# Two output-norm weights moved from every block's gate into the rows of the output projection

## The chip, the cores and the metric

The kernel runs on one core of one Trainium2 chip, in one launch. The metric is the device time of that launch in microseconds (us). The engines of the core are named as the profile names them: PE (matrix products and transposes; PEld is its weight load), DVE (vector engine), ACT (activation engine), POOL (general engine) and SP, whose queue issues this kernel's DMAs.

## The reference, cut to what matters

One hybrid decoder layer over 4096 rows of width 1024. Eight attention heads of width 64 attend in three dilated windows; four heads of width 128 run a gated linear recurrence. Both halves are normalised head by head, multiplied by a norm weight of width 512, gated with silu, joined, and multiplied by `w_out`.

```python
proj = _rmsnorm(x, mix_norm_w) @ w_in
aq, ak, av, ag, hq, hf, hi, hg = split(proj)          # 512 columns each
attn = _longnet_mixture(aq, ak, av)                   # windows (128,1), (512,4), (2048,16)
rec = _hgrn2_chunked(silu(hq), 1 - f, hi, log(f))     # f from hf
y_attn = _head_rmsnorm(attn, attn_out_norm_w, 8) * silu(ag)
y_hgrn = _head_rmsnorm(rec, hgrn_out_norm_w, 4) * silu(hg)
mixed = concatenate([y_attn, y_hgrn], axis=-1)
x = x + mixed @ w_out
return _rmsnorm(x, final_norm_w)
```

A weight that multiplies column c of `mixed` can as well multiply row c of `w_out`.

## The kernel before, in words

`NB` is 32 blocks of 128 rows. Every full-precision product is made of three products of split operands: a high part rounded by ACT (names `hi`, `whi`, `xs`, `ph`) and the rest, `lo`, by DVE or POOL.

Stage 1 (from the start to about 746 us) projects x onto the columns of attention, in two passes P=0 and P=1 over 16 pairs of blocks. `plain_w` and `summed_w` load and combine the weights of a pass, `load_unit` the rows of a pair, and `plain_products` and `unit_rows` form a 2x2 block product from seven `half` products (L725 to L727) with sums on DVE in between (L752 to L763; u2, u4, C0 and C1 are their results). `attn_rows` then, for each block, rotates q and k, splits v, transposes q and k, and makes the gate: `e` is silu of the gate columns, multiplied at L286 by `gv`, a copy of the attention norm weight on all partitions (tile gvA, loaded by a DMA at L787 once for each pass), and written to `sg_d`.

Stage 2 (746 to about 2286 us) projects onto the columns of the recurrence. `for g in range(4, 8)` goes over its four heads and, inside, 16 pairs of blocks; `project_T` and `project_N` make the products (L201), `hgrn_gates`, `hgrn_values` and `hgrn_pair` the recurrence. `hgrn_values` ends with the gate's silu and, at L340 on POOL, a product with `hvec[0]` (tile gv0H, loaded at L295 for each head). Between these steps `take(left + rate)` draws pieces from the generator `attention()`: for each of eight heads the passes d=16, d=4 and d=1, each made of scores (L425, L426), exponentials (L436, L438), transposes (`flip`, L448 to L452), products with v (`weigh`, L460) and, after the pass d=1, `finish`, which reads back the gates from `sg_d`.

Behind that, in the order of the program: the loads of a half of `w_out` (`split_wo` on eight pieces of 128x512, L860 and L861); the rest of attention (`take(10 ** 9)`); 12 early products of the output projection (L878 to L892, `AHEAD`), which need the recurrence's half of `mixed` alone; then stage 3 (about 2398 us to the end): `load_y` reads `mixed` back and transposes it, `summed_wo` loads `w_out` whole (eight pieces `r[j]` of 128x1024 in tile xr, four buffers) and combines it into T1 to T4 and B22 through `split_wo`, and `begin`, `finish_pair` and `final_norm` make the output. T2, T1, T3 and T4 lie in the buffers of QS, KH, KL and OA, which attention's last head reads and writes.

The order in which the instructions stand on each engine is not that of the program. A scheduler plays the program through a modelled timeline and emits each engine's instructions in the order that comes out, bounded by the number of buffers of each tile (`bufs=`). An edit in one place can so move instructions in others.

Of the kernel before, what the change touches and what calls it, by code (L numbers as in the profile page):

```python
# [17 lines left out]
F32 = mybir.dt.float32  # L18
F32R = mybir.dt.float32r
I32 = mybir.dt.int32  # L20
U8 = mybir.dt.uint8
AF = mybir.ActivationFunctionType
ALU = mybir.AluOpType
# [7 lines left out]
KT = 8  # L31
# [4 lines left out]
C1 = 6.28125  # L36
# [13 lines left out]
def layer(ctx: ExitStack, tc: tile.TileContext, x, xT, xP, pos, w_in, w_out, nw, anw, hnw, lbraw, fnw,  # L50
          ident_in, mask_in, trih_in, invf_in, out):
    nc = tc.nc
    V, A, G, T = nc.vector, nc.scalar, nc.gpsimd, nc.tensor
# [16 lines left out]
    mask = const.tile([128, 3, 256], F32, name="mask")  # L70
    caus = const.tile([128, 128], U8, name="caus")
    nwt = const.tile([128, KT], F32, name="nwt")
    nnwt = const.tile([128, KT], F32, name="nnwt")
    mid = ExitStack()
    wp = mid.enter_context(tc.tile_pool(name="wp", bufs=8))
# [7 lines left out]
    rstdn = const.tile([128, NB], F32, name="rstdn")  # L83

    dma(nwt, nw)
    V.tensor_scalar(nnwt, nwt, -1.0, None, op0=ALU.mult)

    def rotary_tables():
# [162 lines left out]
        A.activation(e, e, AF.Ln)  # L251
        A.activation(e, e, AF.Exp, scale=-1.0)

    def attn_rows(P, b, C, gv):

        bs = slice(b * 128, (b + 1) * 128)
        t2 = p1p.tile([128, 2, 4, 16], F32, name="rot")
        c = C[:, :, 0:256].rearrange("p g (q e) -> p g q e", q=4)
        for n in range(2):
            sn = rsin[:, b : b + 1, 8 * n : 8 * n + 8].unsqueeze(1).to_broadcast([128, 2, 4, 8])  # L260
            V.tensor_mul(t2[:, :, :, 8 * n : 8 * n + 8], c[:, :, :, 8 - 8 * n : 16 - 8 * n], sn)
        c16 = c[:, :, :, 0:16]
        V.tensor_mul(c16, c16, rcos[:, b : b + 1, :].unsqueeze(1).to_broadcast([128, 2, 4, 16]))
        V.tensor_add(c16, c16, t2)
        hl = p1p.tile([128, 2, 2, 128], F32R, name="hl")
        rv = C[:, :, 256:384].rearrange("p g (q e) -> p g q e", q=2)
        V.tensor_copy(hl[:, :, :, 0:64], rv)
        G.tensor_tensor(hl[:, :, :, 64:128], rv, hl[:, :, :, 0:64].bitcast(F32), op=ALU.subtract)
        for g in range(2):
            dma(v_d[2 * P + g][bs], hl[:, g].bitcast(F32))  # L270
        pt_ = ps_x.tile([128, 512], F32, name="tr")
        for g in range(2):
            for q in range(2):
                T.transpose(pt_[:, g * 256 + q * 128 : g * 256 + (q + 1) * 128], C[:, g, q * 128 : (q + 1) * 128], ident)
        st = p1p.tile([128, 2, 4, 128], F32R, name="stk")
        p4 = pt_.rearrange("p (g n c) -> p g n c", g=2, n=2)
        A.activation(st[:, :, 0:2], p4, AF.Copy)
        V.tensor_sub(st[:, :, 2:4], p4, st[:, :, 0:2].bitcast(F32))
        for g in range(2):
            dma(qk_d[2 * P + g][:, :, bs], st[:, g].bitcast(F32))  # L280

        e = p1p.tile([128, 2, 128], F32, name="sg")
        A.activation(e, C[:, :, 384:512], AF.Exp, scale=-1.0)
        sigm(e)
        V.tensor_mul(e, e, C[:, :, 384:512])
        V.tensor_mul(e, e, gv)  # L286
        dma(sg_d[bs, P * 256 : (P + 1) * 256], e.rearrange("p g c -> p (g c)"))


# [1 line left out]

    def load_vec(pool, p):
        c = slice(p * 128, (p + 1) * 128)
        v0 = pool.tile([128, 128], F32, name="gv0H", bufs=1)
        dma(v0, hnw[:, c].partition_broadcast(128))  # L295
        v1 = pool.tile([128, 2], F32, name="gv1", bufs=2)
        dma(v1[:, 0:1], omlb_d[:, c].rearrange("o c -> c o"))
        V.tensor_scalar(v1[:, 1:2], v1[:, 0:1], -1.0, None, op0=ALU.mult)
        return v0, v1

    def hgrn_gates(t, ps):

        omlb, nomlb = hvec[1][:, 0:1], hvec[1][:, 1:2]
        rb = hp.tile([128, 256], F32, name="hrb", bufs=1)
        dma(rb, rstd_d[:, t * 256 : (t + 1) * 256].partition_broadcast(128))
        z = hp.tile([128, 2, 256], F32, name="hz", bufs=1)
        e = hp.tile([128, 2, 256], F32, name="he", bufs=1)
        V.tensor_tensor(z, ps.rearrange("p (a c) -> p a c", a=2), rb.unsqueeze(1).to_broadcast([128, 2, 256]), op=ALU.mult)  # L308
        A.activation(e, z, AF.Exp, scale=-1.0)
        sigm(e)  # L310
        G.tensor_tensor(z[:, 1], z[:, 1], e[:, 1], op=ALU.mult)
        cum = hp.tile([128, 256], F32, name="hcum", bufs=1)
        A.activation(cum, e[:, 0], AF.Ln, scale=nomlb, bias=1.0)
        V.tensor_tensor_scan(cum, keep, cum, 0.0, op0=ALU.mult, op1=ALU.add)
        c2 = cum.rearrange("p (n c) -> p n c", n=2)
        V.scalar_tensor_tensor(c2, c2[:, :, 127:128].to_broadcast([128, 2, 128]), -0.5, c2, op0=ALU.mult, op1=ALU.add)
        ea = hp.tile([128, 256], F32, name="hea", bufs=2)
        A.activation(ea, cum, AF.Exp)
        A.activation(cum, cum, AF.Exp, scale=-1.0)
        qd = hp.tile([128, 256], F32, name="hqd", bufs=2)  # L320
        G.tensor_tensor(qd, z[:, 1], ea, op=ALU.mult)
        kd = hp.tile([128, 256], F32, name="hkd", bufs=2)
        V.scalar_tensor_tensor(kd, e[:, 0], omlb, cum, op0=ALU.mult, op1=ALU.mult)
        return qd, kd, ea

    def hgrn_values(t, ps):

        n0 = 2 * t % 4
        if n0 == 0:
            hst["gv"] = hp.tile([128, 4, 256], F32, name="hgv", bufs=2)  # L330
            hst["ss"] = hp.tile([128, 4], F32, name="hss", bufs=2)
        gv = hst["gv"][:, n0 : n0 + 2]
        for n in range(2):
            b = 2 * t + n
            A.activation(gv[:, n], ps[:, 256 * n : 256 * (n + 1)], AF.Copy, scale=rstdn[:, b : b + 1])
        e = hp.tile([128, 2, 128], F32, name="heg", bufs=1)
        A.activation(e, gv[:, :, 0:128], AF.Exp, scale=-1.0)
        sigm(e)
        G.tensor_tensor(gv[:, :, 0:128], gv[:, :, 0:128], e, op=ALU.mult)
        G.tensor_tensor(gv[:, :, 0:128], gv[:, :, 0:128], hvec[0].unsqueeze(1).to_broadcast([128, 2, 128]), op=ALU.mult)  # L340

    def hgrn_pair(hh, t, qd, kd, ea):

# [396 lines left out]
        A.activation(C0[:, 0], pa, AF.Copy, scale=rstd[:, 2 * t : 2 * t + 1])  # L740
        return u2, pe

    def unit_rows(P, t, X, W, gv, C0, begun):
        u2, pe = begun
        b0, b1 = 2 * t, 2 * t + 1
        C1 = p1p.tile([128, 2, 512], F32, name="C", bufs=3)
        if pe is None:
            pe = ps_m.tile([128, 512], F32, name="m")
            half(pe, X["S4"], W["B22"])
        pb = ps_m.tile([128, 512], F32, name="m")  # L750
        half(pb, X["S2"], W["T2"])
        V.tensor_tensor(u2, pb, u2, op=ALU.add)  # L752
        pc = ps_m.tile([128, 512], F32, name="m")
        half(pc, X["S1"], W["T1"])
        u4 = p1p.tile([128, 512], F32, name="u4", bufs=1)
        V.tensor_tensor(u4, pc, u2, op=ALU.add)
        V.tensor_tensor(C0[:, 1], pe, u4, op=ALU.add)
        A.activation(C0[:, 1], C0[:, 1], AF.Copy, scale=rstd[:, b0 : b0 + 1])
        pd = ps_m.tile([128, 512], F32, name="m")
        half(pd, X["S3"], W["T3"])  # L760
        V.tensor_tensor(C1[:, 1], pd, u4, op=ALU.add)
        half(pd, X["A22"], W["T4"], start=False)
        V.tensor_tensor(C1[:, 0], pd, u2, op=ALU.add)  # L763
        A.activation(C1, C1, AF.Copy, scale=rstd[:, b1 : b1 + 1])
        attn_rows(P, b0, C0, gv)
        attn_rows(P, b1, C1, gv)

    def row_tile():
        return p1p.tile([128, 2, 512], F32, name="C", bufs=3)
# [12 lines left out]
    for P in range(2):  # L782
        if P:
            W = {"B11": plain_w(1, 0), "B21": plain_w(1, 1)}
            summed_w(1, W)
        gv = p1p.tile([128, 2, 128], F32, name="gvA", bufs=1)
        dma(gv, anw[:, P * 256 : (P + 1) * 256].rearrange("o (g c) -> o g c", g=2).partition_broadcast(128))  # L787
        early = None
        for t in range(NB // 2):
            if not P and t != 1:  # L790
# [8 lines left out]
            if (P, t) == (0, 0):  # L799
                row_stats(1)  # L800
                C0n = row_tile()
                early = C0n, plain_products(1, Xn, W, C0n, third=False)
            unit_rows(P, t, X, W, gv, C0, begun)
            X = Xn
            if (P, t) == (0, 3):
                lower_bounds()
# [33 lines left out]
    X = load_pair(0, 4)  # L840
# [15 lines left out]

    def split_wo(raw, hi, lo):
        A.activation(hi, raw, AF.Copy)  # L860
        V.tensor_sub(lo, raw, hi.bitcast(F32))  # L861
        return hi, lo

    WO = {}
    for j in range(2):
        WO[f"B{j + 1}1"] = []
        for k in range(4 * j, 4 * j + 4):
            raw = xp.tile([128, 512], F32, name="raw", bufs=3)
            dma(raw, w_out[k * 128 : (k + 1) * 128, 0:512])
            WO[f"B{j + 1}1"].append(split_wo(raw, wp.tile([128, 512], F32R, name="whi", bufs=8),  # L870
                                             wp.tile([128, 512], F32R, name="wlo", bufs=8)))
    three.close()
    fp = two.enter_context(tc.tile_pool(name="fp", bufs=1))
    fnwt = fp.tile([128, D], F32, name="fnwt", bufs=1)
# [118 lines left out]
    def summed_wo():  # L993
        bt = {n: big.tile([128, S], F32R, name="w" + n, tag=tag) for n, tag in (("T2", "QS"), ("T1", "KH"), ("T3", "KL"), ("T4", "OA"))}
        WO.update({n: [None] * 4 for n in ("T1", "T2", "T3", "T4", "B22")})
        for k in range(4):
            r = [fp.tile([128, D], F32, name="xr", bufs=4) for _ in range(2)]
            for j in range(2):
                dma(r[j], w_out[(4 * j + k) * 128 : (4 * j + k + 1) * 128, :])
            b11, b12, b21, b22 = r[0][:, c0], r[0][:, c1], r[1][:, c0], r[1][:, c1]  # L1000

            def unit(name, src):
# [78 lines left out]
```

## Time and profile before

| what | value |
|---|---|
| three runs | 2721.2, 2730.94, 2735.6 us; median 2730.94 |
| the profiled execution: its time, its span | 2725.64 us, 2723.9 us |
| mean granted PE clock | 0.968 of full speed |
| busy PE, DVE, ACT, POOL | 2559.8, 2042.7, 1743.4, 1066.0 us |
| DMA, share of 16 engines | 60.1% |

The span runs from the first to the last instruction that the profile shows; 1.7 us of the execution lie around it. The busy times are sums over the whole span, with stages of different limits in it. Times in the rows below are in us from the start of the span; a row of windows has the window, its length, then for PE, PEld, DVE, ACT and POOL the busy time with the number of instructions, the granted PE clock, the share of DMA engines busy, and GB/s.

### The profile page before, as it was taken

The numbers are of one execution on the slowest core, as the hardware profiler recorded it, in microseconds if no ns is written. First come the engines' busy times: TensorE is split into PE (matmuls) and PEld (weight loads), VectorE is DVE, ScalarE is ACT, GpSimd is POOL, SyncE is SP. The second block draws the span as 40 slices with busy tenths as digits, with TensorE's granted clock in tenths as the row PEclk, the third lists the DMA queues.
The fourth block names the chain that finished last, engine by engine and source line by source line (L and its number), as shares of the span: only waits on it lengthen the run. The fifth ranks groups of instructions, "written<-read, shape, count | busy, mean of one in ns | idle before, by whom it ended". The sixth has DMA issues, their size and how long they took to land. (4 is left out here: it accounts for less than half of the span.)

```text
span 2723.9 us, 52124 instructions
## 1 busy us (share of the span) xinstructions
PE 2559.8 (94%) x17186; PEld 2310.5 (85%) x17186; DVE 2042.7 (75%) x5322; ACT 1743.4 (64%) x4811; POOL 1066.0 (39%) x1012
## 2 busy tenths in 40 slices
PE   5899989999979999999999899999899999889998
PEld 4678867888879989899999799999899998668886
DVE  8787788777637788777787787677787877867875
ACT  8755565555548768768667677577678677534443
POOL 5455646665434364142242141231231331144443
PEclk8999999999979999999999899999999998999999
DMA  6864463444686775774774764764855753645553
GB/s 230 257 180 143 150 205 114 150 147 143 184 271 185 222 244 175 201 188 135 199 202 143 214 178 136 208 173 148 239 168 151 227 160 103 202 151 181 182 159 109
DMA packets 459106, 487.44 MB, mean 179 GB/s; under 512 B 120105, under 2 KB 335189, under 8 KB 458837
## 3 DMA queue, kind: packets, MB, share of 16 engines
q1 hardware_dynamic: 458836, 484.12, 60.1%
q8 instruction: 137, 2.24, 0.3%
q14 instruction: 133, 1.08, 0.1%
HBM read 354.45 MB, written 129.52 MB: 178 GB/s over the span
## 5 line engine op out<-in xcount | busy, mean ns | idle before, releaser
L201 PE MATMUL proj<-xs,whi 128*128 128x256 f32 x2048 | 432.1, 296 | 20.9 <-ACT whi L163 12.3
L201 PE MATMUL proj<-whi,xs 128*128 128x256 f32 x2048 | 431.9, 293 | 3.7 <-DVE hz L308 3.7
L201 PEld LDWEIGHTS proj<-xs,whi 128*128 128x128 f32 x2048 | 333.9, 194 | 27.2 <-ACT whi L163 13.7
L201 PEld LDWEIGHTS proj<-whi,xs 128*128 128x128 f32 x2048 | 335.3, 193 | 5.3 <-DVE hz L308 3.9
L436 DVE CUSTOM_DVE_ANT_0 pt<-att,mask 128x256 f32<-128x256 f32 (+1 forms) x768 | 269.2, 387 | 76.4 <-PE att L426 74.6
L201 PE MATMUL proj<-xs,wlo 128*128 128x256 f32 x1024 | 302.0, 295 | 0.3 <-DVE wlo L164 0.3
L201 PE MATMUL proj<-wlo,xs 128*128 128x256 f32 x1024 | 299.9, 293 | 0.0
L452 DVE TENSOR_TENSOR pl<-att,ph 128x512 fp32r<-128x512 f32 (+1 forms) x384 | 237.4, 624 | 55.4 <-ACT ph L451 53.0
L438 ACT ACTIVATE pt<-pt,ml 128x256 f32<-128x256 f32 (+1 forms) x512 | 238.1, 467 | 55.3 <-DVE ml L436 54.2
L451 ACT ACTIVATE ph<-att 128x512 fp32r<-128x512 f32 (+1 forms) x384 | 203.4, 542 | 50.5 <-PE po L460 24.3
L448 PE MATMUL att<-ident,pt 128*128 128x128 f32 x1368 | 227.7, 279 | 4.2 <-ACT pt L438 3.0
L460 PE MATMUL po<-ph,vh 128*128 128x128 f32 (+1 forms) x856 | 211.9, 277 | 8.4 <-ACT ph L451 2.6
L460 PE MATMUL po<-pl,vh 128*128 128x128 f32 (+1 forms) x856 | 206.4, 287 | 1.3 <-DVE pl L452 1.2
L201 PEld LDWEIGHTS proj<-xs,wlo 128*128 128x128 f32 x1024 | 199.0, 194 | 2.1 <-issue 1.2
L201 PEld LDWEIGHTS proj<-wlo,xs 128*128 128x128 f32 x1024 | 198.0, 193 | 1.2 <-issue 1.0
L460 PEld LDWEIGHTS po<-ph,vh 128*128 128x128 f32 x856 | 166.5, 194 | 13.0 <-issue 5.4
L466 ACT ACTIVATE pot<-po 64x512 f32<-64x512 f32 (+1 forms) x256 | 124.2, 485 | 73.7 <-DVE o L570 34.2
L725 PE MATMUL m<-tw,ss 128*128 128x512 f32 x384 | 155.0, 404 | 16.9 <-ACT tw L172 6.6
L448 PEld LDWEIGHTS att<-ident,pt 128*128 128x128 f32 x1368 | 161.7, 143 | 9.6 <-ACT pt L438 5.0
L460 PEld LDWEIGHTS po<-pl,vh 128*128 128x128 f32 x856 | 167.0, 195 | 2.8 <-DVE pl L452 2.3
L726 PE MATMUL m<-tw,ss 128*128 128x512 f32 x384 | 154.9, 404 | 4.7 <-DVE tw L173 4.7
L727 PE MATMUL m<-tw,ss 128*128 128x512 f32 x384 | 155.9, 406 | 0.0
(313 smaller groups left out, 7721.9 us busy)
## 6 DMA issues: line engine op xcount, KB each, us to landing
xs<-xh_d SPq DMA_DIRECT2D x192, 512.0 KB
xr<-xT SPq DMA_DIRECT2D x128, 256.0 KB
qk_d<-stk SPq DMA_DIRECT2D x128, 256.0 KB
xh_d<-xs SPq DMA_DIRECT2D x64, 512.0 KB
vh<-v_d SPq DMA_DIRECT2D x512, 64.0 KB
raw<-x SPq DMA_DIRECT2D x76, 256.0 KB
v_d<-hl SPq DMA_DIRECT2D x128, 128.0 KB
raw<-xP SPq DMA_DIRECT2D x64, 256.0 KB
```

Source lines behind the costliest of these rows:

```text
L201: m = T.matmul(o, l, r, start=first is None, stop=(k == KT - 1 and g == len(groups) - 1 and n == 2))
L436: V.tensor_tensor_reduce(out=p_, in0=o, in1=mask[:, (1, 4, 16).index(d), 256 - 128 * nk : 256], scale=-0.125, scalar=3e38, op0=ALU.add, op ...
L438: A.activation(p_, p_, AF.Exp, scale=-1.0, bias=m, accum_out=l)
L448: T.transpose(ps[:, n * 128 : (n + 1) * 128], loc[u], ident)
L451: A.activation(ph[:, :w], ps[:, :w], AF.Copy)
L452: V.tensor_sub(pl[:, :w], ps[:, :w], ph[:, :w].bitcast(F32))
L460: T.matmul(po[:, 128 * c : 128 * (c + n)], v, rh, start=(s == 0), stop=(s == len(steps) - 1))
L466: A.activation(t[o : o + 64, c], po[64 - o : 128 - o, c], AF.Copy)
L725: T.matmul(ps, hi[:, c], whi, start=start and k == 0, stop=False, skip_group_check=not start)
L726: T.matmul(ps, hi[:, c], wlo, start=False, stop=False, skip_group_check=not start)
L727: T.matmul(ps, lo[:, c], whi, start=False, stop=(k == 3), skip_group_check=not start)
```

## The change

The weights of both norms are loaded once as columns (`onw`, 128 partitions by 8, from two small DMAs), with the host laying out `anw` and `hnw` as 4 columns each. `attn_rows` loses its product with `gv` and the pass its DMA; `hgrn_values` loses its product with `hvec[0]` and the head its DMA (`hvec` is now what was `hvec[1]`). `split_wo` takes a scale: the eight early pieces of `w_out` are scaled while they are split. In `summed_wo` each piece of 128x1024 is scaled in place by ACT before it is combined.

```diff
+    onw = const.tile([128, KT], F32, name="onw")
...
     dma(nwt, nw)
+    dma(onw[:, 0:4], anw)
+    dma(onw[:, 4:8], hnw)
...
         V.tensor_mul(e, e, C[:, :, 384:512])
-        V.tensor_mul(e, e, gv)
...
     def load_vec(pool, p):
         c = slice(p * 128, (p + 1) * 128)
-        v0 = pool.tile([128, 128], F32, name="gv0H", bufs=1)
-        dma(v0, hnw[:, c].partition_broadcast(128))
...
         G.tensor_tensor(gv[:, :, 0:128], gv[:, :, 0:128], e, op=ALU.mult)
-        G.tensor_tensor(gv[:, :, 0:128], gv[:, :, 0:128], hvec[0].unsqueeze(1).to_broadcast([128, 2, 128]), op=ALU.mult)
...
-        gv = p1p.tile([128, 2, 128], F32, name="gvA", bufs=1)
-        dma(gv, anw[:, P * 256 : (P + 1) * 256].rearrange("o (g c) -> o g c", g=2).partition_broadcast(128))
...
-    def split_wo(raw, hi, lo):
-        A.activation(hi, raw, AF.Copy)
-        V.tensor_sub(lo, raw, hi.bitcast(F32))
+    def split_wo(raw, hi, lo, s=None):
+        if s is None:
+            A.activation(hi, raw, AF.Copy)
+            V.tensor_sub(lo, raw, hi.bitcast(F32))
+        else:
+            A.activation(hi, raw, AF.Copy, scale=s)
+            V.scalar_tensor_tensor(lo, raw, s, hi.bitcast(F32), op0=ALU.mult, op1=ALU.subtract)
...
-                                             wp.tile([128, 512], F32R, name="wlo", bufs=8)))
+                                             wp.tile([128, 512], F32R, name="wlo", bufs=8), onw[:, k : k + 1]))
...
                 dma(r[j], w_out[(4 * j + k) * 128 : (4 * j + k + 1) * 128, :])
+                A.activation(r[j], r[j], AF.Copy, scale=onw[:, 4 * j + k : 4 * j + k + 1])
...
-        "anw": np.ascontiguousarray(attn_out_norm_w[0].reshape(1, 512)),
-        "hnw": np.ascontiguousarray(hgrn_out_norm_w[0].reshape(1, 512)),
+        "anw": np.ascontiguousarray(attn_out_norm_w[0].reshape(4, 128).T),
+        "hnw": np.ascontiguousarray(hgrn_out_norm_w[0].reshape(4, 128).T),
```

The emitted order changes with it. On SP's queue, at the start of the program, the rows before are these (each is one kind of DMA, the tile written, and what is read; nwt holds the input norm's weights, C the angles of the rotary tables, raw and xr the first weights and rows):

```order
L85 DMA nwt<-nw 128x8
L92 DMA C<-pos 128x32
L93 DMA C<-invf_in 128x8
L154 DMA raw<-w_in 128x512 x3
L699 DMA xr<-xT 128x512 x4
```

And the rows of the changed kernel at that place:

```order
L86 DMA nwt<-nw 128x8
L87 DMA onw<-anw 128x4
L88 DMA onw<-hnw 128x4
L95 DMA C<-pos 128x32
L96 DMA C<-invf_in 128x8
L157 DMA raw<-w_in 128x512 x3
L698 DMA xr<-xT 128x512 x4
```

The two new DMAs stand ahead of everything but the input norm's weights.

On PE, at the end of stage 2, behind the last projection: the place is near the end of the 12 early products (`proj<-whi,xs 128x512`, with the transposes `hp` ahead of each). In the rows before, the tenth of them stands between the scores (`att<-KH,QS`), transposes (`att<-ident,pt`) and products with v (`po`) of the last pass, d=1, of the last head, which reads its queries from QS itself:

```order
L425 MATMUL att<-KH,QS 128x256
L426 MATMUL att<-KL,QS 128x256
L448 MATMUL att<-ident,pt 128x128 x11
L885 MATMUL hp_32176<-ident,raw 128x128 x4
L460 MATMUL po<-ph,vh 128x256
L448 MATMUL att<-ident,pt 128x128 x4
L460 MATMUL po<-pl,vh 128x256
L460 MATMUL po<-ph,vh 128x256
L605 MATMUL att<-ident,OA 128x128 x2
L725 MATMUL proj<-whi,xs 128x512
L726 MATMUL proj<-wlo,xs 128x512
```

In the changed kernel the end of the twelfth early product is followed by the rest of the pass d=4 of that head, whose queries are the copy `qc`:

```order
L724 MATMUL proj<-whi,xs 128x512
L725 MATMUL proj<-wlo,xs 128x512
L726 MATMUL proj<-whi,xs 128x512
L447 MATMUL att<-ident,pt 128x128 x7
L424 MATMUL att<-KH,qc 128x256
L425 MATMUL att<-KL,qc 128x256
L424 MATMUL att<-KH,qc 128x256
L425 MATMUL att<-KL,qc 128x256
L459 MATMUL po<-ph,vh 128x256
L459 MATMUL po<-pl,vh 128x256
```

The early products moved from the last pass to the passes ahead of it, and the pass d=1 now stands alone. Counted over the whole of PE's order, 495 products and transposes stood between the last projection (L201) and the first product of stage 3 (`att<-whi,xs`, L725), and 917 stand there now; the 422 more are all attention, which stood between the projections of stage 2 before.

On ACT, near the end of the last pass, the rows before are the exponentials' followers (`ph`, `pot`) and the high parts of the combined weights (L860; wT and ph):

```order
L451 ACTIVATE ph<-att 128x512
L860 ACTIVATE wT_32313<-xr 128x512
L451 ACTIVATE ph<-att 128x384
L860 ACTIVATE ph<-xr 128x512
L466 ACTIVATE pot<-po 64x256
L860 ACTIVATE wT_32312<-u_32367 128x512
L860 ACTIVATE wT_32314<-xr 128x512
```

And of the changed kernel at that place:

```order
L450 ACTIVATE ph<-att 128x512
L1001 ACTIVATE xr<-xr,onw 128x1024
L450 ACTIVATE ph<-att 128x384
L1001 ACTIVATE xr<-xr,onw 128x1024
L858 ACTIVATE ph<-xr 128x512
L465 ACTIVATE pot<-po 64x256
L858 ACTIVATE wT_32176<-xr 128x512
```

Four of the eight scalings (L1001) stand earlier, beside the early products, two here, and two some ten rows later.

More of the change, by code (lines that the diff above doesn't have):

```diff
@@ L252, in sigm, with attn_rows @@
         A.activation(e, e, AF.Exp, scale=-1.0)
-    def attn_rows(P, b, C, gv):
+    def attn_rows(P, b, C):
         bs = slice(b * 128, (b + 1) * 128)
@@ L298, in load_vec @@
         V.tensor_scalar(v1[:, 1:2], v1[:, 0:1], -1.0, None, op0=ALU.mult)
-        return v0, v1
+        return v1
     def hgrn_gates(t, ps):
-        omlb, nomlb = hvec[1][:, 0:1], hvec[1][:, 1:2]
+        omlb, nomlb = hvec[:, 0:1], hvec[:, 1:2]
         rb = hp.tile([128, 256], F32, name="hrb", bufs=1)
@@ L741, in plain_products, with unit_rows @@
         return u2, pe
-    def unit_rows(P, t, X, W, gv, C0, begun):
+    def unit_rows(P, t, X, W, C0, begun):
         u2, pe = begun
@@ L764, in unit_rows @@
         A.activation(C1, C1, AF.Copy, scale=rstd[:, b1 : b1 + 1])
-        attn_rows(P, b0, C0, gv)
-        attn_rows(P, b1, C1, gv)
+        attn_rows(P, b0, C0)
+        attn_rows(P, b1, C1)
     def row_tile():
@@ L802, in layer @@
                 early = C0n, plain_products(1, Xn, W, C0n, third=False)
-            unit_rows(P, t, X, W, gv, C0, begun)
+            unit_rows(P, t, X, W, C0, begun)
             X = Xn
```

## The prediction

> **What bounds the kernel now.** I read the page first (sums, slices), then one table of windows cut by stage, then PE's waits.
>
> ```profile
> span 2723.9 us, 52124 instructions
> PE 2559.8 (94%) x17186; PEld 2310.5 (85%) x17186; DVE 2042.7 (75%) x5322; ACT 1743.4 (64%) x4811; POOL 1066.0 (39%) x1012
> PE   5899989999979999999999899999899999889998
> DVE  8787788777637788777787787677787877867875
> ```
>
> PE is busy for 94% of the span and sits near 9 tenths all through; its idle 164 us (2723.9 − 2559.8) are gathered in a few slices of 68 us: the first two, the sixth (340 to 408), the twelfth (749 to 817, where stage 2 begins; the change touches one DMA there) and the 35th and 36th. The windows show what the others are: the start, the change of weights between the two passes of stage 1, and the end of stage 2; and a change of heads in stage 2.
>
> ```profile
> 0.00:150.00 150.00, 111.72 (x425) 85.50 (x426) 120.51 (x265) 115.95 (x284) 71.19 (x55) 0.89 0.76 242
> 150.00:375.00 225.00, 220.84 (x1006) 181.99 (x1005) 176.43 (x311) 121.01 (x230) 133.26 (x111) 0.99 0.51 155
> 375.00:435.00 60.00, 46.19 (x158) 31.72 (x158) 52.36 (x80) 38.64 (x69) 27.48 (x18) 0.86 0.52 164
> 435.00:746.00 311.00, 307.90 (x1458) 254.81 (x1456) 231.42 (x421) 163.76 (x304) 178.03 (x148) 1.00 0.50 154
> 1160.00:1515.00 355.00, 351.38 (x2959) 342.37 (x2959) 269.43 (x857) 260.15 (x815) 102.86 (x124) 0.99 0.62 173
> 1518.00:1542.00 24.00, 20.08 (x147) 17.07 (x148) 20.94 (x79) 16.46 (x55) 2.67 (x3) 0.97 0.83 228
> 2286.23:2398.36 112.13, 92.56 (x507) 75.82 (x506) 89.54 (x242) 61.52 (x172) 17.24 (x15) 0.86 0.59 182
> 2310.00:2398.00 88.00, 73.18 (x389) 58.93 (x390) 71.64 (x182) 43.80 (x116) 15.05 (x12) 0.90 0.66 203
> ```
>
> In the steady windows of stages 1 and 2 PE is busy 98 to 99%: there an instruction taken from DVE or POOL buys nothing, and one added costs nothing. In 0 to 150, 375 to 435, at the change of heads (1518 to 1542, attention alone on PE) and from the last projection to the first product of stage 3 (2286.23 to 2398.36, below "the tail") PE has 16 to 26% free, and DVE with 80 to 87% is the busiest of the others. That is where the change can act.
>
> **The change part by part.**
>
> *The start.* Two DMAs more stand on SP ahead of the first loads; the interval between such issues is 1.19 − 0.73 = 0.46 us.
>
> ```profile
> 0.73 0.40 SPq L85 DMA_DIRECT2D nwt<-nw  x1
> 1.19 0.42 SPq L92 DMA_DIRECT2D C<-pos  x1
> ```
>
> All first loads come 2 x 0.46 = 0.9 us later: +0.9 (ends 0, if DMA bandwidth sets the start, and +0.9). The two DMAs that leave L787 and the four that leave L295 free SP of as many issues at places where PE is 98% busy: 0.
>
> *L286, 64 products on DVE.* They sum to 53.7 us.
>
> ```profile
> L286 DVE TENSOR_TENSOR sg<-sg,gvA 128x256 f32<-128x256 f32 x64 | 53.7, 839 | 2.0
> L286 DVE TENSOR_TENSOR sg<-sg,gvA x64: 408/426/1518, 69.2 to 741.4; 128x256 f32<-128x256 f32 x64
> PE m L725 <- DVE C L761: 15.5, 7, 4.3
> 80.17 1.45 DVE L286 TENSOR_TENSOR sg<-sg,gvA 128x256 f32<-128x256 f32 x1
> 81.54 0.68 DVE L757 TENSOR_TENSOR C<-m,u 128x512 f32<-128x512 f32 x1
> 376.88 1.52 DVE L286 TENSOR_TENSOR sg<-sg,gvA 128x256 f32<-128x256 f32 x1
> 378.32 0.68 DVE L752 TENSOR_TENSOR u<-m,u 128x512 f32<-128x512 f32 x1
> ```
>
> PE's wait for DVE's sums (L761) is 15.5 us in 7 waits. In the two windows of stage 1 in which PE is not full I found L286 twice directly ahead of a sum in that line, at 80.17 and 376.88; the sums behind begin 1.37 and 1.44 us later than they need. I take these two: −2.8. The other 62 lie beside PE that is 98 to 99% busy: 0. Ends: 0, and −15.5 if every L761 wait goes. If the wait goes, the products' own order is what is next.
>
> The row of L286 has a median of 426 ns and a maximum of 1518: some of these products are held up. The Trainium skill ("SBUF — State Buffer", section "Who interferes with whom") says that a DVE instruction with two inputs in SBUF contends with a POOL instruction that reads SBUF, and that the first to start blocks the other for its whole length. The spread agrees; by that rule the POOL work that held L286 might hold the next DVE instruction instead, but L757 and L752 read one input from PSUM, so the sum by the rule stays −2.8.
>
> *L340, 64 products on POOL.* POOL is at 29% in the steady window of stage 2 (102.86 of 355).
>
> ```profile
> L340 POOL TENSOR_TENSOR hgv<-hgv,gv0H 128x256 f32<-128x256 f32 x64 | 47.9, 748 | 3.6
> PE att L425 <- POOL qc L410: 5.4, 1, 5.4
> PE proj L201 <- POOL xs L173: 1.5, 2, 0.8
> ```
>
> 47.9 us leave POOL under a PE at 99%; I take 0. PE's waits for POOL in this stage sum to 5.4 + 1.5 = 6.9, of which one is 5.4: ends 0 and −6.9.
>
> *split_wo with a scale.* ACT's form with a scale takes 714 ns against 629, DVE's scalar_tensor_tensor 1068 against 695.
>
> ```profile
> L860 ACT ACTIVATE whi<-raw 128x512 fp32r<-128x512 f32 x8 | 4.9, 629 | 1.6 <-DMA raw<-w_out 1.6
> L676 ACT ACTIVATE C<-C,nwt 128x512 f32<-128x512 f32 x24 | 16.4, 714 | 3.7 <-DMA C<-w_in 3.7
> L861 DVE TENSOR_TENSOR wlo<-raw,whi 128x512 fp32r<-128x512 f32 x8 | 5.5, 695 | 1.1 <-ACT whi L860 1.1
> L660 DVE SCALAR_TENSOR_TENSOR wlo<-raw,nwt,whi 128x512 fp32r<-128x512 f32 x16 | 16.9, 1068 | 4.5 <-ACT whi L659 4.5
> ```
>
> 8 x 0.085 = 0.7 us on ACT and 8 x 0.373 = 3.0 on DVE. They fall beside attention's products: 0; ends 0 and +3.0, if DVE bounds that place.
>
> *Eight scalings of 128x1024 on ACT.* Nearest row: the same form at L764, 1144 ns.
>
> ```profile
> L764 ACT ACTIVATE C<-C,rstd 128x1024 f32<-128x1024 f32 x32 | 36.6, 1144 | 6.2 <-DVE C L763 6.2
> 2396.62 0.67 DVE L861 TENSOR_TENSOR wT<-xr,wT 128x512 fp32r<-128x512 f32 x1
> 2398.36 0.48 PE L725 MATMUL att<-whi,xs 128*128 128x512 f32 x1
> 2416.93 0.39 PE L725 MATMUL att<-wT,pt 128*128 128x512 f32 x1
> ```
>
> 8 x 1.144 = 9.2 us. ACT is busy 43.8 of 88 us in the window where the weights are combined, so it has room; the last combined weight is ready at 2396.62 + 0.67 = 2397.3, and the first product that reads one starts at 2416.93: 19.6 us of slack. I take 0; without that cover the end is +9.2.
>
> *The moved attention.* 422 products leave the projections' phase, where PE is full: by the window 1160 to 1515 (2959 in 355 us, 8.34 a us) that phase shortens by 422 / 8.34 = 50.6 us. They come to the tail, where PE is not the bound. Attention alone (1518 to 1542) needs 20.94 us of DVE for 147 products, 0.142 each: 422 x 0.142 = 60.1 us. The tail then has 89.54 + 60.1 = 149.6 us of DVE work. How densely does DVE run it? The tail before runs at 89.54 / 112.13 = 80%; attention alone at 20.94 / 24 = 87%. What is added is attention alone, so I take 87%: 149.6 / 0.8725 = 171.5 us, against 112.1 + 50.6 = 162.7 for the same work before: +8.8. Ends: at 80% 187.0, that is +24.3; at a full DVE 149.6, −13.1.
>
> The clock matters here: it is granted at 0.97 in 1518 to 1542, at 0.90 in 2310 to 2398, against 0.99 to 1.00 in the steady windows. The Trainium skill ("TensorE: Matmul & The Clock Gate", "Part 1: The HAM clock gate") says that PE falls to half its clock after about 3.4 us of idleness and needs as long of work to come back. The rows agree in kind; by that rule a longer tail with more gaps would lie nearer to the 80% end, +24.3.
>
> **Sum:** +0.9 − 2.8 + 0 + 0 + 0 + 8.8 = +6.9 us. The profiled execution took 2725.6 (span 2723.9 and 1.7 around it), so 2732.5 on its scale. It lies 5.3 below the median of the three runs, 2730.94; on the median's scale the forecast is 2737.8. A measurement of this kernel can tell 0.5%, 13.7 us, from no change (the three runs lie 14.4 apart): faster ends at 2717.3, slower begins at 2744.6.
>
> **The rivals.**
>
> *Slower: the tail stays as sparse as it was.* The pass d=1 of the last head stands alone, with no early products in its gaps, and each score waits for the mask, the exponential, the transpose, the split. For it speaks the tail before: 80% with early products to fill it. At the pace of attention alone counted in products (147 in 24.00 us, 6.13 a us), with the tail's own part unchanged, the 422 take 68.9 us: 68.9 − 50.6 = +18.3; at 80% it is +24.3. With −1.9 for the rest: 2747 to 2753, 2750 in the middle. It decides from a moved term over 15.6 (13.7 + 1.9), a tail longer than 162.7 + 15.6 = 178.3 us, a DVE share under 84%. Against it: the added share ran at 87%.
>
> *Slower: the scaled weights come late.* The scalings wait for a DMA and lengthen the chain through the four buffers of xr; if the 19.6 us of slack are gone because the last head now ends later, 9.2 come on top: 2737.8 + 9.2 = 2747. For it: four of the five combined weights are written into buffers that the last head reads. Against it: four scalings stand among the early products, long before.
>
> *Faster: DVE's relief carries stage 1, and the moved work costs nothing.* All L761 waits go (15.5), and with them the waits of the transposes for rotated rows:
>
> ```profile
> PE tr L274 <- DVE C L264: 4.9, 3, 4.3
> ```
>
> 15.5 + 4.9 = 20.4; with the moved term at 0 and +0.9 for the start: 2730.9 − 20.4 + 0.9 = 2711.4. For it: DVE is busy 80 and 87% of the windows 0 to 150 and 375 to 435. Against it: only two of the 64 products stood in a late line.
>
> **How the numbers follow.** The forecast (within 0.5% of before) 0.46; sparse tail 0.28; late weights 0.06; faster 0.20. The likeliest is the sum, 2737.8. The range goes from the faster rival, 2711, to the sparse tail's far end with late weights on top, 2753 + 9 = 2762; cases of both signs hold 0.54, and the likeliest one's own range is 2724 to 2745 (moved term from −5 to +16). Faster 0.20, same 0.46, slower 0.34.
>
> **What would show it.** In the profile after: the tail, from the last L201 product to the first product of `att<-whi,xs`, near 171 us and holding some 920 products, its DVE share near 87%; the stretch of stage 2 ahead of it shorter by about 50 us; stage 1 shorter by 2 or 3 us, with L761's wait still over 10; eight scalings of about 1.14 us each on ACT, and no PE wait for wT or ph that comes from them; POOL's sum down by 48 and DVE's by 51 with PE's sum unchanged. I am wrong if the tail runs at 80% or below, if PE's clock in it falls under 0.8, if stage 1 shortens by 10 us or more, or if stage 2's projections don't get shorter with the attention gone from them.

## The result, and the profile after

The changed kernel takes 2742.31 us in the median of nine runs, against 2722.09 for the kernel before in nine runs. The ratio, which here and below is estimated over the runs and is not that of the medians, is 1.0057, 95% interval 1.0043 to 1.0071: some 15.5 us slower, where the medians lie 20.2 us apart. The ratios leave out runs over 1.5% above the fastest of their kernel: two of e1_one_dma's six (2869.08 and 4123.12 us), one of e8_spread_16's twelve (6353.92) and one of the kernel before in the series of e5 to e8 (11794.53). The forecast was +6.9 us and no change that can be told; its sign was right, its size short by half. The profiled execution took 2743.19 us.

The sums of the page went much as written down: DVE 2042.7 to 1986.0 us (down 56.7, forecast 51), POOL 1066.0 to 1017.4 (down 48.6, forecast 48), PE nearly unchanged. The span is longer all the same.

```profile
span 2741.2 us, 52083 instructions
PE 2553.7 (93%) x17186; PEld 2309.2 (84%) x17186; DVE 1986.0 (72%) x5258; ACT 1752.8 (64%) x4819; POOL 1017.4 (37%) x948
PE   5899989999979999999999999999999979679998
```

In the slices, the weak place of PE ahead of stage 3 has grown from two slices of 8 tenths to slices of 7, 9, 6 and 7. Windows cut at the first and the last product of stage 2's projections and at the first product of stage 3 show where the time went. First before (stage 1, the projections' phase, the last 20 us of the tail, stage 3), then after (with the whole tail as the third row, its last 20 us as the fourth):

```profile
0.00:732.60 732.60, 674.17 (x2942) 541.98 (x2942) 572.06 (x1050) 430.51 (x867) 407.87 (x327) 0.96 0.55 172
732.60:2286.20 1553.60, 1488.58 (x12289) 1441.28 (x12290) 1149.68 (x3602) 1120.68 (x3448) 488.32 (x554) 0.97 0.65 188
2378.40:2398.40 20.00, 14.28 (x62) 10.71 (x60) 17.92 (x37) 9.30 (x20) 2.33 (x2) 0.83 0.69 204
2398.40:2723.90 325.50, 304.38 (x1452) 251.38 (x1450) 231.41 (x431) 130.62 (x326) 152.55 (x116) 0.99 0.51 152
```

```profile
0.00:733.20 733.20, 672.81 (x2943) 543.24 (x2943) 523.50 (x988) 432.39 (x869) 404.90 (x327) 0.96 0.56 171
733.20:2200.80 1467.60, 1417.54 (x11865) 1377.98 (x11866) 1068.54 (x3371) 1057.51 (x3252) 419.08 (x464) 0.99 0.67 193
2200.80:2413.30 212.50, 155.61 (x935) 135.05 (x933) 160.40 (x471) 131.34 (x374) 40.81 (x41) 0.82 0.45 134
2393.30:2413.30 20.00, 6.58 (x26) 5.02 (x26) 16.21 (x34) 13.05 (x24) 2.64 (x2) 0.50 0.59 170
2413.30:2741.20 327.90, 307.70 (x1446) 252.88 (x1446) 233.60 (x431) 131.56 (x326) 152.62 (x116) 0.97 0.50 150
```

Stage 1 gained nothing (732.6 to 733.2). The projections' phase is 86.0 us shorter (1553.6 to 1467.6), the tail 100.3 us longer (112.2 to 212.5), stage 3 2.4 longer: 0.6 − 86.0 + 100.3 + 2.4 = +17.3, the difference of the spans. In the tail PE is busy 73% and DVE 75%, and in the last 20 us PE does a third of what it could, at a granted clock of 0.50. The Trainium skill ("TensorE: Matmul & The Clock Gate", "Part 1: The HAM clock gate") says that PE is set to half its clock after an idle window of some 3.4 us. The window's 0.50 is that half; the idle time is not seen so: the clock was down to 0.50 by 2379 us, and PE's longest gap in the ten us ahead of that was 1.55 us.

### The profile page after: what moved, and what is told of

The parts are those of the page before. It is cut to its first block, busy times and chain, and to the rows that moved or that the text cites. A ratio compares the mean times of both kernels' runs of the same rounds, so it can differ in the third digit from the quotient of the medians.

```text
span 2741.2 us, 52083 instructions
## 1 busy us (share of the span) xinstructions
PE 2553.7 (93%) x17186; PEld 2309.2 (84%) x17186; DVE 1986.0 (72%) x5258; ACT 1752.8 (64%) x4819; POOL 1017.4 (37%) x948
## 4 chain that ended last, share of the span: by engine, by line
PE 62%; DVE 13%; DMA 11%; ACT 6%; issue 4%; POOL 2%; SPq 2%; POOLq 0%; DVEq 0%; ACTq 0%
PE proj L204 17%; PE m L724 6%; PE m L725 6%; PE m L726 6%; PE po L459 5%; PE att L447 4%; PE att L424 3%; PE att L425 3%; DMA y_d<-pr 2%; PE att L724 2%; PE att L726 2%; PE att L725 2%; DMA raw<-x 1%; ACT pt L437 1%; DMA QS<-qk_d 1%
## 5 line engine op out<-in xcount | busy, mean ns | idle before, releaser
L204 PE MATMUL proj<-whi,xs 128*128 128x256 f32 x2048 | 437.6, 293 | 8.5 <-DVE hz L308 8.5
L204 PE MATMUL proj<-xs,whi 128*128 128x256 f32 x2048 | 425.1, 293 | 14.4 <-DVE hz L308 5.4
L204 PEld LDWEIGHTS proj<-whi,xs 128*128 128x128 f32 x2048 | 335.7, 192 | 10.8 <-DVE hz L308 9.0
L450 ACT ACTIVATE ph<-att 128x512 fp32r<-128x512 f32 (+1 forms) x384 | 202.4, 541 | 55.8 <-PE att L447 28.4
L725 PE MATMUL m<-tw,ss 128*128 128x512 f32 x384 | 152.9, 398 | 3.1 <-DVE tw L176 3.1
```

What stands on the lines that cost most here:

```text
L204: m = T.matmul(o, l, r, start=first is None, stop=(k == KT - 1 and g == len(groups) - 1 and n == 2))
L450: A.activation(ph[:, :w], ps[:, :w], AF.Copy)
L725: T.matmul(ps, hi[:, c], wlo, start=False, stop=False, skip_group_check=not start)
```

## The experiments

Four questions: is it the work or the order; what in the order; what do the scalings cost; and can the loss be had back. The table has for each kernel the products that its emitted order puts into the tail (before and after counted with one end more than the others), where among them the last early product begins, the lengths of the phases in its one profile, and the ratio of its runs to runs of the kernel before on the same chip.

| kernel | products in tail | last early product at | projections, tail, stage 3 (us) | ratio to before, 95% interval |
|---|---|---|---|---|
| before | 495 | 96% | 1553.6, 112.2, 325.5 | |
| after | 917 | 61% | 1467.6, 212.5, 327.9 | 1.0057 (1.0043 to 1.0071) |
| e1_one_dma | 925 | 69% | 1473.7, 208.4, 326.9 | 1.0056 (1.0042 to 1.0070) |
| e12_two_dmas | 847 | 76% | 1468.5, 184.8, 326.6 | 0.9974 (0.9961 to 0.9987) |
| e2_removal | 941 | 70% | 1466.6, 214.4, 326.5 | 1.0039 (1.0026 to 1.0052) |
| e3_adds | 847 | 76% | 1472.6, 186.1, 328.7 | 0.9980 (0.9966 to 0.9993) |
| e4_held | 409 | 95% | 1569.2, 103.6, 318.5 | 0.9997 (0.9982 to 1.0012) |
| e5_spread | 912 | 98% | 1461.4, 208.8, 325.8 | 1.0014 (1.0002 to 1.0025) |
| e6_no_scaling | 916 | 64% | 1467.8, 205.8, 326.0 | 1.0013 (1.0000 to 1.0025) |
| e7_held_16 | 473 | 96% | 1564.8, 123.1, 312.6 | 1.0039 (1.0023 to 1.0054) |
| e8_spread_16 | 982 | 97% | 1460.4, 211.0, 314.5 | 0.9994 (0.9981 to 1.0006) |
| e9_pool | 930 | 68% | 1464.4, 204.4, 317.4 | 0.9978 (0.9966 to 0.9990) |
| e10_pool_spread_16 | 982 | 97% | 1468.1, 206.8, 316.7 | 0.9988 (0.9974 to 1.0001) |
| e11_pool_held | 409 | 95% | 1566.3, 106.6, 319.3 | 1.0015 (1.0004 to 1.0027) |

The phases of one profile carry an uncertainty of their own. In after, e5, e6, e8, e9 and e10 every engine's order is the same up to the last projection; yet their projections' phase took 1460.4 to 1468.1 us. Differences of a phase under 8 us between two profiles are not read.

**e1_one_dma and e12_two_dmas: no work, another order.**

```diff
     dma(nwt, nw)
+    onw = const.tile([128, KT], F32, name='onw')
+    dma(onw, nw)                      # e1_one_dma
+    dma(onw[:, 0:4], nw[:, 0:4])      # e12_two_dmas, in place of the line above
+    dma(onw[:, 4:8], nw[:, 4:8])
```

> The kernel before, with one more DMA of 128x8 on SP at the start whose data nobody reads; no other work changes. The scheduler's order changes with it: 925 products stand between the last projection and stage 3, against 495. Order theory (the 15 us lost are the price of the order, attention left for the tail): 0.4 to 0.8% slower than before (10 to 22 us), the tail over 200 us, stage 2's projections ending some 85 us earlier. Work theory (the loss comes from what the change adds, scalings and DMAs): within 0.1% of before, at most 0.5 us for the DMA.

> The kernel before with two DMAs of 128x4 on SP at the start whose data nobody reads, and nothing else: the order on PE is that of e3_adds up to the tail (847 products in it). e3_adds was 0.2% faster than before and e1_one_dma, with one such DMA, 0.56% slower. If the order alone made both: this kernel is at e3_adds (-0.2%) or, by the scalings that it lacks, up to 10 us faster still. If e3_adds was fast for another reason (what it adds): this kernel is slower than before by 0.3% or more, like e1_one_dma.

One DMA of 4 KB that nobody reads made the kernel 0.56% slower, as much as the whole change; two of 2 KB made it 0.26% faster. The windows of e1_one_dma have the shape of after: 

```profile
733.30:2207.00 1473.70, 1423.74 (x11863) 1382.65 (x11864) 1073.50 (x3373) 1054.01 (x3245) 465.10 (x528) 0.98 0.67 193
2207.00:2415.40 208.40, 155.17 (x939) 134.21 (x937) 157.87 (x473) 124.12 (x373) 41.07 (x41) 0.83 0.48 139
2395.40:2415.40 20.00, 5.49 (x25) 4.48 (x25) 15.72 (x34) 8.73 (x18) 2.30 (x2) 0.56 0.59 166
```

and those of e12_two_dmas have a tail of 184.8 us with the same PE-poor end:

```profile
2203.30:2388.10 184.80, 142.56 (x861) 122.94 (x859) 143.02 (x425) 115.71 (x347) 31.21 (x33) 0.83 0.47 141
2368.10:2388.10 20.00, 7.37 (x29) 5.14 (x29) 17.83 (x35) 9.61 (x20) 2.64 (x2) 0.50 0.61 174
```

The order alone so moves this kernel over some 0.8%, wider than the effect that was asked about.

**e2_removal and e3_adds: the change's two halves.** The first leaves out the loads of `onw` and both uses of it, so that the norm weights are missing from its result; the second is the kernel before with loads, scalings and scaled splits added and both gate products kept, so that the weights are applied twice.

> The changed kernel without anything that the change adds: no loads of onw, no scalings; both norm weights are left out of the result. It is work taken away alone, 102 us of DVE and POOL. Its order has 941 products in the tail. Order theory: slower than before all the same, by 0.3 to 0.8% (8 to 20 us). Work theory: faster than or equal to before, and faster than the changed kernel by the scalings, 5 to 15 us.

> The kernel before with everything that the change adds and nothing taken away: the gates keep their products, and the weights are applied a second time in the output projection. 847 products stand in the tail. Order theory: slower than before by 0.3 to 0.7%, like the changed kernel though it keeps 102 us of work more. Work theory (additions cost, removals give): clearly slower than the changed kernel, by 5 us or more.

Taking 102 us of DVE and POOL work away made the kernel 0.39% slower; adding the scalings and taking nothing away made it 0.20% faster. The work theory has both signs wrong. The order theory, as I had put it (more products in the tail, more time), missed e3_adds as well: 847 products in the tail and no loss. e12_two_dmas, with e3_adds' order on PE up to 22 products ahead of the tail and none of its work, is as fast: what is good in e3_adds is its order. The tail of e3_adds is shorter than e1_one_dma's by 22.3 us with 78 products fewer, and its projections' phase is no longer (1472.6 against 1473.7). Why that order packs more densely I did not settle.

What the emitted order shows of the cause in the kernel before: on SP's queue the last weights of stage 2's second and third head (`raw<-w_in`) stand behind 30 loads of the next attention head (ten each of `KH`, `KL`, `QS`). The projections then stand still and attention catches up: 104 and 142 of its products lie between two projections. In after the weights stand ahead of these loads, the longest such gap in the projections of these heads is 30 products, and attention is left over for the end. The profile shows the one as a gap in PE at a change of heads, which is gone in after (before, then after). No run here undid that alone, and it does not tell the slow orders from the fast ones: in e1_one_dma, e3_adds and e12_two_dmas, too, no such gap is longer than 30 products.

```profile
1515.00:1548.00 33.00, 21.89 (x155) 17.86 (x153) 22.19 (x82) 18.20 (x61) 6.62 (x7) 0.89 0.83 231
```

```profile
1515.00:1548.00 33.00, 33.00 (x278) 32.38 (x279) 22.30 (x72) 25.20 (x73) 3.67 (x5) 1.00 0.60 170
```

**e4_held: the changed kernel with attention held beside the projections.**

```diff
-            qd, kd, ea = hgrn_gates(t, project_T(X, W))
+            past.append(hst.get('pv'))     # the last product with v drawn so far
+            qd, kd, ea = hgrn_gates(t, project_T(X, W, past[-13] if len(past) > 12 else None))
...
                     if first is None:
                         first = m
+                        if hold:
+                            after(m, hold)
```

> The changed kernel with its whole arithmetic, and one rule of order: on PE the first product of a block pair's projection may not stand ahead of the last product with v that was drawn 12 pairs earlier. 409 products stand in the tail instead of 917. Order theory: back to before or below it, between -0.5% and +0.2%, with a tail near 100 us. Work theory: stays near the changed kernel's +0.57%, since no work changes. Should holding the projections open new gaps in stage 2, the gain is smaller: PE would then be under 96% busy between 1160 and 2200 us.

0.9997: with the change's whole arithmetic the loss is gone. But the gain in the tail (212.5 to 103.6 us) came with a price in the projections' phase (1467.6 to 1569.2), where PE is busy 1496 of 1569 us, 95%:

```profile
734.80:2304.00 1569.20, 1496.09 (x12380) 1447.48 (x12381) 1135.82 (x3648) 1131.38 (x3489) 441.05 (x491) 0.98 0.65 186
2304.00:2407.60 103.60, 79.75 (x422) 61.55 (x421) 82.83 (x205) 59.12 (x141) 21.70 (x18) 0.92 0.68 208
```

**e5_spread: fillers kept for the last pass.** The transposes of early products 5 to 12 wait for one group of attention's last eight products with v each; nothing else changes.

```diff
-            T.transpose(pt_[:, c], yt[:, c], ident)
+            m = T.transpose(pt_[:, c], yt[:, c], ident)
+            if k == 0 and (t - 12 if t > 3 else 0) < 0:
+                after(m, pvs[(t - 12 if t > 3 else 0)])
```

> The changed kernel with its arithmetic and its order of stage 2 (912 products in the tail), and one rule: early products 5 to 12 may not stand on PE ahead of the last eight groups of products with v, one each. They so end at 98% of the tail's products instead of 61%. If the loss is that attention's last pass runs without filler: 8 to 15 us under the changed kernel, that is 0.0 to +0.3% against before, the tail under 205 us, and PE busy over 12 us of the last 20 ahead of stage 3 (6.6 in the changed kernel). If it is the amount of attention left for the tail, wherever the fillers stand: within 3 us of the changed kernel, near +0.5%.

11.9 us under the changed kernel by the medians (2730.38 against 2742.31), inside what the filler theory gave, with as much attention in the tail. PE does twice the work in the last 20 us:

```profile
2384.60:2404.60 20.00, 12.84 (x48) 9.71 (x49) 17.39 (x35) 12.50 (x24) 2.85 (x2) 0.72 0.63 190
```

The tail, 208.8 us, is only 3.7 shorter in these two profiles, not the 7.5 that I had written; that is under what one profile can tell. Of the 10.8 us between the two spans 6.2 lie in the projections' phase, where the order is the same. So the runs show the gain, and the profiles do not show that the tail made it.

**e6_no_scaling and e9_pool: what the scalings cost.** The first takes the eight scalings in `summed_wo` away, the second puts them on POOL:

```diff
-                A.activation(r[j], r[j], AF.Copy, scale=onw[:, 4 * j + k : 4 * j + k + 1])
+                G.tensor_scalar(r[j], r[j], onw[:, 4 * j + k : 4 * j + k + 1], None, op0=ALU.mult)   # e9_pool
```

> The changed kernel without the eight scalings of 128x1024 in the combination of the output weights (the norm weights are left out of that part of the result); the order on PE is the same up to the tail, 916 products in it. Cover theory (the scalings lie in ACT's free time, the combined weights are ready some 19 us before they are read): within 3 us of the changed kernel. Late-weights theory: 4.6 to 9.2 us faster than the changed kernel, +0.2 to +0.4% against before.

> The changed kernel with the eight scalings of the output weights on POOL in place of ACT; the same arithmetic. In the changed kernel's tail the scalings wait on ACT for their DMA (5.1 us in 3 waits), and attention's own ACT instructions stand behind them. If that is why the kernel without the scalings was 12 us faster: 5 to 12 us faster than the changed kernel, 0.1 to 0.4% above before, and ACT's waits for xr<-w_out gone. If it is the length of the chain from the DMA to the combined weights, which grows on POOL (about 3 us a scaling, from POOL's 748 ns for a quarter of the size): no faster than the changed kernel, +0.5% or more.

Without the scalings (the norm weights are then missing from that part of the result) the kernel is at 1.0013, 0.44% or some 12 us under the changed kernel; the two intervals leave room for 7 to 17, so that it is more than the 9.2 us that they last is not shown. The weights were not late: the last `wT` is ready at 2413.6 + 0.7 = 2414.3 and first read at 2433.2, 18.9 us of slack (forecast: 19.6).

```profile
L859 DVE TENSOR_TENSOR wT<-xr,wT x12: 670/675/1662, 2383.6 to 2413.6; 128x512 fp32r<-128x512 f32 x12
L724 PE MATMUL att<-wT,pt x128: 387/389/487, 2433.2 to 2726.0; 128*128 128x512 f32 x128
```

What they do is stand in the lines of engines. The group's idle time and rows of ACT near the tail's end, in after:

```profile
L1001 ACT ACTIVATE xr<-xr,onw 128x1024 f32<-128x1024 f32 x8 | 9.2, 1146 | 7.6 <-DMA xr<-w_out 5.1 <-DVE o L569 2.4
```

```profile
2388.42 0.59 ACT L450 ACTIVATE ph<-att 128x512 fp32r<-128x512 f32 x1
2391.42 1.15 ACT L1001 ACTIVATE xr<-xr,onw 128x1024 f32<-128x1024 f32 x1 [2.41 <-DMA xr<-w_out]
2392.47 0.47 ACT L450 ACTIVATE ph<-att 128x384 fp32r<-128x384 f32 x1
```

A scaling waits 2.41 us for its piece of `w_out`, and attention's own split (`ph`, L450) stands behind it: from 2388.42 + 0.59 = 2389.0 to 2392.47 ACT gives the last pass nothing. But that wait is not what the tail ended on. The longer pieces of the chain that ended last in the tail of after, from 2389 on (start, length, what it ran on):

```profile
2389.16 4.62 DMA xr<-w_out
2393.80 1.16 ACT xr L1001
2397.80 3.00 DVE wT L859 x5
2400.84 4.46 DMA xr<-w_out
2405.66 1.16 ACT xr L1001
2411.59 1.20 DVE wT L859 x2
2412.79 0.48 DVE pr L607
2413.31 0.79 PE att L724
```

The first product of stage 3 waits for `pr`, the last head's own work on DVE, and `pr` stands in DVE's line behind the sums and splits of the weights, which wait for the scalings, and these for their DMAs. e6_no_scaling has this chain without the two scalings, and is no quicker through it: 23.8 us from the start of that DMA to the product (2382.16 to 2405.94) against 24.2 here. The 6.6 us that its tail is shorter, less than one profile can tell, were made earlier. The 31st product with v begins 37.1 us into the tail of after and 37.5 into that of e6_no_scaling, the 62nd at 67.7 and 61.4, the last, the 244th, at 203.8 and 197.2. Between the 31st and the 62nd the chain of after runs through sums of the first scaled weights, which stand in one block on DVE ahead of attention's `pt`:

```profile
2254.83 1.26 DVE L1009 TENSOR_TENSOR xr<-xr 128x512 f32<-128x512 f32 x1
2256.19 1.57 DVE L1011 TENSOR_TENSOR u<-xr 128x512 f32<-128x512 f32 x1
2257.68 1.09 DVE L1014 TENSOR_TENSOR xr<-xr 128x512 f32<-128x512 f32 x1
2258.70 0.28 DVE L435 CUSTOM_DVE_ANT_0 pt<-att,mask 128x128 f32<-128x128 f32 x1
```

In e6_no_scaling they take 0.68 us each and attention's instructions stand between them. So in these two profiles the scalings cost by what they delay into DVE's line rather than by ACT's; no run here isolates it.

On POOL, busy 19% of this tail, a scaling takes 2.5 times as long or more and still waits for its DMA. No other engine is seen waiting for it, but on POOL itself the last head's `pr` stands behind one, on the chain that ended last (the third and fourth row):

```profile
2239.00 2.85 POOL L1001 TENSOR_SCALAR xr<-xr,onw 128x1024 f32<-128x1024 f32 x1 [4.42 <-DMA xr<-w_out]
2378.81 5.70 POOL L1001 TENSOR_SCALAR xr<-xr,onw 128x1024 f32<-128x1024 f32 x2 [5.47 <-DMA xr<-w_out]
2387.96 3.51 POOL xr L1001
2391.47 2.69 POOL pr L619
2195.90:2400.30 204.40, 155.81 (x950) 133.67 (x948) 159.05 (x469) 123.94 (x369) 68.50 (x51) 0.84 0.48 141
```

e9_pool is at 0.9978, faster than the kernel before and 0.79% (1 − 0.9978/1.0057), some 21 us, under the changed one with the same arithmetic: more than I expected of it. It gained 8.1 us in the tail and 10.5 in stage 3 by the profiles. All of that can't be the scalings' price: e6_no_scaling, which has none of them, lies 0.35% or some 9.5 us above e9_pool, clear of both intervals. That part is order. One place shows it: 14 transposes of stage 3 stand ahead of its first product in e9_pool, in the tail (930 products against 916), and PE is busy 29.5 us of stage 3's first 30 (the second row; the first is after):

```profile
2413.31:2443.31 30.00, 24.15 (x97) 19.49 (x98) 15.93 (x28) 10.82 (x21) 15.81 (x13) 0.81 0.38 123
2400.26:2430.26 30.00, 29.52 (x128) 24.00 (x129) 25.38 (x42) 12.70 (x27) 20.59 (x16) 0.90 0.40 125
```

The orders of after, e6_no_scaling and e9_pool are the same up to the tail, but inside it they differ, so how much of e6_no_scaling's 12 us is the scalings and how much order stays open too.

**e7, e8, e10, e11: combinations.** Sixteen early products in place of twelve (`AHEAD = 16`), with the hold of e4_held or spread over attention's last 16 groups; then the scalings of e8_spread_16 and of e4_held on POOL.

> The changed kernel with the projections held to 12 pairs behind attention as in e4_held, and 16 early products of the output projection instead of 12. The four more put 64 products into the tail (473 in all) and take 48 of 0.227 us, 10.9 us, out of stage 3, which is full. If the tail has room for them: 3 to 8 us faster than e4_held, -0.1 to -0.3% against before. If DVE bounds the tail: each costs 1.4 us of DVE there, 5.5 in all, and the gain is under 5 us or none.

> The changed kernel with 16 early products, each held behind one of attention's last 16 groups of products with v, and nothing held in stage 2 (982 products in the tail). Filler theory: faster than e5_spread by the 5 us or so that stage 3 loses, -0.2 to +0.1% against before. If the amount of attention in the tail decides: near the changed kernel, +0.3 to +0.6%.

> e8_spread_16 with the scalings on POOL. If the two repairs add up: 5 to 10 us faster than before, -0.2 to -0.4%. If the fillers already cover what the scalings hold up: as e8_spread_16, -0.06%, within 3 us.

> e4_held with the scalings on POOL (409 products in the tail). If the scalings cost by holding up attention's instructions on ACT, and early products fill the gaps there: within 3 us of e4_held (-0.03%). If they cost by themselves, 5 to 10 us faster: -0.2 to -0.4% against before.

e8_spread_16 came out as the filler theory had it: 0.9994, with 982 products in a tail no longer than after's (211.0 us against 212.5) and stage 3 13.4 us shorter (327.9 to 314.5). e7_held_16 missed: 1.0039, slower than e4_held, its tail 19.5 us longer against 5.9 saved in stage 3; its profiled execution, 2731.44 us, was the fastest of its nine, whose median is 2739.74, and what separates these I can't say. e10_pool_spread_16 is at 0.9988, as forecast for the case that they do not add up, within 3 us of e8_spread_16; it is not faster than e9_pool either. That fits two repairs of the same idle time, which no profile here shows. e11_pool_held, 1.0015, is not faster than e4_held but 0.18% or 4.9 us slower, beyond the 3 us that I had written, though the intervals overlap. It speaks against scalings that cost by themselves; why it is slower I did not settle.

## Why the prediction was right or wrong

**The bound.** Right: the steady windows give nothing back. 53.7 us left DVE in stage 1 and 47.9 left POOL in stage 2, and stage 1 ended where it had, 0.6 us later. For POOL no run isolates it, since attention moved out of the same phase.

**The start, +0.9.** Right in place and size: PE's first product came at 14.15 us, against 13.14.

```profile
13.14 0.77 PE L725 MATMUL m<-whi,xs 128*128 128x512 f32 x1 [13.14 <-SPq L775]
14.15 0.76 PE L724 MATMUL m<-whi,xs 128*128 128x512 f32 x1 [14.15 <-SPq L774]
```

**L286, −2.8.** Not found. PE's wait for that sum (0 to 735 us) went up, not down:

```profile
PE m L724 <- DVE C L760: 23.5, 7, 5.4
```

It was 15.5. Of the two places that I had counted one gained, the sum at 378.32 now beginning at 376.54; the other did not (81.87 against 81.54), since other instructions stand ahead of it there now.

```profile
81.87 0.69 DVE L756 TENSOR_TENSOR C<-m,u 128x512 f32<-128x512 f32 x1
376.54 0.68 DVE L751 TENSOR_TENSOR u<-m,u 128x512 f32<-128x512 f32 x1
```

In ten kernels without L286 (after, e2 and e4 to e11) the first projection came between 729.2 and 734.8 us; before had it at 732.6. A gain of 2.8 us is inside that spread, so the term is at most a few us of either sign; the rival's 20.4, which was to end stage 1 so much sooner, did not come.

**L340, 0, and split_wo, 0.** Nothing in the profiles speaks against them; no run isolates L340. Of the bound of 3.0 us for DVE there was 0.4 to pay, 8 x (751 − 695): the 1068 that I took is the mean of a row with a few long ones, and the median of that row was 750.

```profile
L861 ACT ACTIVATE whi<-raw,onw x8: 706/716/725, 2197.2 to 2209.4; 128x512 fp32r<-128x512 f32 x8
L862 DVE SCALAR_TENSOR_TENSOR wlo<-raw,onw,whi x8: 733/751/752, 2198.0 to 2211.9; 128x512 fp32r<-128x512 f32 x8
```

**The scalings, 0.** The price was right (1146 ns against 1144), and the weights had the slack that I gave them or nearly; the step that failed is that I asked only which products wait for the scaled weights, not what stands behind the scalings on ACT and behind the weights' sums on DVE. In the profile after it is attention's `pt` at 2258.70 and the last head's `pr` at 2412.79, which holds the first product of stage 3. I also took the slack at the wrong reader: `att<-ph,qc` reads the combined weight B22 already at 2412.9 in before, 16.5 us after its last split and not 19.6 (17.3 in after). The late-weights rival named the longer chain through the buffers of `xr`, which is there, but expected products to wait for weights, and PE's waits in stage 3 name none; that its 2747 lies near 2742.31 is luck. What the scalings cost is not shown beyond the 12 us of e6_no_scaling, a part of which may be order.

**The moved attention, +8.8.** The count was right (917 in the tail), and so was what it does to the two phases; both sizes were off and partly cancelled, and the step that failed is the density of the tail. The projections' phase shortened by 86.0 us, not 50.6: I priced the 422 products at the pace of a full window. PE's idle time there fell by 15.0 us (65.0 to 50.1), since some of them had run at the changes of heads, where PE had been a third idle; its busy time fell by 71.0, and the granted clock of the phase rose from 0.97 to 0.99, of which I had said nothing.

The tail grew by 100.3 us, not 59.4. Its DVE work is 160.40 us where I had 149.6, and its DVE share 160.40 / 212.50 = 75%, under the 80% of before, where I took 87%: at 87% the work would have taken 183.8 us, so the density is worth 28.7 us of the 41 missing and the amount the rest. A share of 80% or below was one of my signs of being wrong. It is the sparse-tail rival, beyond its points of 84% and 178.3 us, with +14.3 us net just short of its 15.6 and under its +18 to +24. The argument against it was that the added work had run at 87% by itself; the rival had it right that the fillers do not stay where the attention is: they went to the first 61% of the tail, and the last pass and the combination of weights stood alone. e5_spread puts them back and its runs gain 11.9 us.

**The whole.** The likeliest case was the wrong one of two neighbours; the measured 0.57% lies just past the border of 0.5% that I had drawn between them. In absolute time 2737.8 is 4.5 us from the measured 2742.31, and that is luck: it stood on a median of three runs, 2730.94, and the median of nine is 8.9 us lower. The terms for the change's own work explain nothing of the loss, since e1_one_dma has none of that work and the same loss. The one term of the right kind was the moved attention, and it was too small.

## What to carry to other kernels

Where a scheduler sets the order, compare the emitted order before pricing an edit, and run the kernel before with an edit that does nothing (a DMA nobody reads): its effect is the noise floor of the comparison, here −0.26% and +0.56%. When an instruction that waits for a DMA is added to an engine, ask what of other work stands behind it in that engine's line, and in the lines of those that wait for it; the same arithmetic on another engine was 0.79% faster here, a good part of it again by order. Work that can fill gaps (the early products) may be worth holding back for the stretch in which nothing else fills them: e5_spread and e8_spread_16 ran 0.43 and 0.63% under the changed kernel.

## What the runs showed of the hardware

Kernels with the same order on every engine up to the last projection took 1460.4 to 1468.1 us from the first projection to it, in one profile each; a phase of a single profile so differs by half a per cent with nothing changed in it. POOL's scaling of 128x1024 by a column took 2.85 to 4.02 us, 3.07 in the median, where ACT's took 1.146 in the mean. The sums of weights on DVE, 128x512, took 0.68 us in e6_no_scaling and 1.26, 1.57 and 1.09 in the block at 2254.83 to 2257.68 of after; no run here shows why.
